# Two loads per head tied to a later store: the x1 loads of a hybrid decoder layer on one Trainium2 core

## The chip, the cores and the metric

The kernel runs on one core of one Trainium2 chip. The metric is device time in microseconds (us). Before the change it was timed three times: 1514.49, 1511.58 and 1510.92 us, median 1511.58 us. The profiled execution, a run of its own, took 1510.96 us.

## The reference

One decoder layer over 1024 tokens of 1024 features in float32. Two groups of heads, a chunked mLSTM and a forgetting attention, run on the same normalised input; their joined result goes through `w_out` and is added to x. Then comes a cross-attention into 256 memory tokens, and then a squared-ReLU MLP, each with its own pre-norm and residual:

```python
x = x + jnp.concatenate([ml_out, fx_out], axis=-1) @ w_out[l]
x = x + cross_attention(rmsnorm(x, ln_x[l]), rmsnorm(mem, ln_mem[l]), w_xq[l], w_xkv[l], w_xo[l])
u = jax.nn.relu(rmsnorm(x, ln2[l]) @ w_ff1[l])
x = x + (u * u) @ w_ff2[l]
return rmsnorm(x, ln_f)
```

In `cross_attention` the queries are `h @ w_q` for four heads of 256 features; keys and values come from the memory tokens; scores, softmax, weighted values and `w_xo` follow. The change touches how the sum of the first line ("x1" below, the first result) gets from DRAM to the place where the queries are made.

## The kernel before

**Layout.** Activations are stored feature-major: a tile is 128 features by 512 tokens. There are 8 feature tiles (KT) and two halves of 512 tokens (`hf` 0 and 1). A float32 product is made of three matmuls: every operand is cut into a high and a low part in the `fp32r` type (`split`, lines 131 to 138: ScalarE copies the high part, VectorE subtracts it to leave the low part), and `mm3` (lines 184 to 188) multiplies low by high, high by low and high by high into one PSUM bank.

**The end of the first result.** `w_out` is applied in two pieces. The first piece is added to x earlier and stored to the DRAM buffer `x1d`. The loop at lines 1139 to 1149 does the second: for `n0` in 0 and 4, for both halves, for four tiles `n`, nine matmuls make one tile in PSUM, and `full_sink` (line 1122) finishes it. It loads the partial sum from `x1d` into a buffer that comes in turn from `p`, `d`, `e` (line 1125), adds the PSUM bank (line 1126), and stores the sum back to the same place of `x1d` (line 1127). For the first half it also cuts the scaled sum into `h2`, which stays in SBUF. For the second half nothing stays in SBUF: the sum is only in `x1d`. `square_sum` adds the squares for the norm. So there are 16 stores; the last four are tiles 4, 5, 6 and 7 of the second half. `mix_done` holds the store of tile 5 (n == KT - 3) of the second half.

**The cross-attention's first half.** The loop at line 1451 runs over the four heads. For each head, `query_whole` multiplies two blocks of `w_xq` by `h2` (24 matmuls each, into the PSUM banks `mm` and `m2`, 512 tokens of the first half) and evicts them with a scaled split into the buffers `b`, `c` or `p`, `a`/`y` (line 1198). `right_side(hd)` prepares the second half, and `cross_head(hd, 0, ...)` does scores, softmax and values for the first half with the keys and values of its head, loaded at lines 1276 and 1277.

**The second half's query combinations.** The queries of the second half are made by a Strassen-like scheme with seven products per pair of blocks (`query_blocks`, line 1231), and these need seven right-hand sides: blocks 11, 21, 22 of the scaled x1 and the combinations t1, t2, t3, t4. `right_side(k)` (line 1168) makes the part of feature tiles k and 4 + k: it loads the two tiles `x` and `y` of x1 from `x1d` (line 1176) into the two buffers of the tag `f`, scales them by `ln_x` on ScalarE (line 1177), cuts three blocks, makes the differences on GpSimd (`sub`, line 1339) in place, and cuts those too; the last difference goes to the tile `fourth`. The four calls, one for each head, use the same two `f` buffers, so each call's loads wait until the one before is done with them. `query_blocks` starts after the loop over the heads and uses all of them.

**Queues and order.** All DMAs named here are issued by SyncE (SP), one after the other: a load whose condition isn't met keeps what stands behind it in SP's queue waiting. The conditions are semaphores put in where data or a buffer is shared; a load from `x1d` waits for the store to the same place to have landed. `tc.issue_after(ins)` is another thing: it waits for nothing by itself, and only says that what is issued in its block stands behind `ins` in the queue of the same engine. Here the order in which an engine gets its instructions is not written out by hand, unlike in the parts under `in_order`: the framework lays out the instructions of every engine when the program is built, with a timing model of its own (`schedule_with_timeline_sim=True`, line 1843). The weights come through the two buffers `wr` (line 174) and are cut into the three buffers each of `wh` and `wl`.

Of the kernel before, what the change touches and what calls it, by code (L numbers as in the profile page):

```python
# [21 lines left out]
KT = D // P  # L22
# [22 lines left out]
def hybrid_layer(ctx: ExitStack, tc: tile.TileContext, a: dict, out: bass.AP):  # L45
# [26 lines left out]
    def w4(shape=(P, 1024), dt=F32):  # L72
        t = sb("w4", [P, 1024], 5, dt)[: shape[0]]
        return t.rearrange("p (a b) -> p a b", b=shape[2]) if len(shape) == 3 else t
# [4 lines left out]
    def w2(tag, n=512, dt=F32, p=P):  # L79
        return sb("r_" + tag, [P, 512], BUFS[tag], dt)[:p, :n]  # L80
# [50 lines left out]
    def split(hi, lo, src, scale=None):  # L131

        if scale is None:
            s.activation(hi, src, AF.Copy)  # L134
            return v.tensor_tensor(out=lo, in0=src, in1=hi.bitcast(F32), op=ALU.subtract)  # L135
        else:
            s.activation(hi, src, AF.Copy, scale=scale)
            return v.scalar_tensor_tensor(out=lo, in0=src, scalar=scale, in1=hi.bitcast(F32), op0=ALU.mult, op1=ALU.subtract)  # L138
# [24 lines left out]
    def rotate(*tags):  # L163

        spare[tags] = spare.get(tags, -1) + 1
        return w2(tags[spare[tags] % len(tags)])
# [52 lines left out]
    def square_sum(acc, x, first, by=s, add=v):  # L219
        sq = acc if first else w2("c")[:, : x.shape[-1]]  # L220
        if by is s:
            s.activation(sq, x, AF.Square)
        else:
            by.tensor_tensor(out=sq, in0=x, in1=x, op=ALU.mult)
        if not first:
            add.tensor_tensor(out=acc, in0=sq, in1=acc, op=ALU.add)
# [872 lines left out]
    n = 0  # L1099
# [14 lines left out]
    banks[:] = ["mm", "tp", "m2", "tp"]  # L1114
    h2 = act(), act()
    x1_accs = [w2("b"), w2("b")]
    mix_done = []

    def ln_x(n):
        return vec[:, VEC["ln_x"] + n :][:, 0:1]  # L1120

    def full_sink(n, hf, ps):
        t = rotate("p", "d", "e")
        with tc.issue_after(last_raw[0].ins):
            load(t, x1d[hf, :, n])
        v.tensor_tensor(out=t, in0=ps, in1=t, op=ALU.add)
        done = load(x1d[hf, :, n], t)
        if hf == 0:
            split(h2[0][:, n], h2[1][:, n], t, ln_x(n))
        square_sum(x1_accs[hf], t, n == 0, add=g)  # L1130
        if hf == 1 and n == KT - 3:
            mix_done.append(done)

    def row_second(hf):
        rsqrt_sums(x1_accs[hf], rcol[:, 4 * hf : 4 * hf + 4], 4)
        if hf:
            to_row(row, rcol, 8, rowd[2:3])

    for n0 in (0, 4):
        ws = [weights(a["w_out_b"][n0 // 2 + i], 6 * P) for i in range(2)]  # L1140
        for hf in range(2):
            for n in range(n0, n0 + 4):
                w = both(ws[n // 2 % 2], lambda t: t.rearrange("p (k c) -> p k c", k=3)[:, :, n % 2 * P : n % 2 * P + P])
                ps = mm()
                for k in range(3):
                    mm3(ps, both(w, lambda t: t[:, k]), mix_fx[hf][k], k == 0, k == 2)
                full_sink(n, hf, ps)
                if hf and n == 6:
                    row_second(0)
# [7 lines left out]
    def right_room(*names):  # L1157
        t = act().rearrange("p a b -> p (a b)").rearrange("p (n q k c) -> p n q k c", n=2, q=2, k=4)
        for e, c in enumerate(names):
            R[c] = t[:, e, 0], t[:, e, 1]  # L1160
        return t[:, 1]

    def cut_right(c, k, x):
        split(R[c][0][:, k], R[c][1][:, k], x)
# [3 lines left out]
    def right_side(k):  # L1168
        if not fourth:
            for c in (("11", "21"), ("t1", "t2"), ("22", "t3")):  # L1170
                right_room(*c)
            fourth.append(w4((P, 4, 256)))
        x, y = w2("f"), w2("f")
        for t, n in ((x, k), (y, 4 + k)):
            with tc.issue_after(mix_done[0].ins):
                load(t, x1d[1, :, n])
            s.activation(t, t, AF.Copy, scale=ln_x(n))
        x1, x2, y1, y2 = (t[:, e * 256 : e * 256 + 256] for t in (x, y) for e in range(2))
        cut_right("11", k, x1)
        cut_right("21", k, y1)  # L1180
        cut_right("22", k, y2)
        sub(x1, x2, x1, g)
        cut_right("t1", k, x1)
        sub(x1, y2, x1, g)
        cut_right("t2", k, x1)
        sub(x2, y2, x2, g)
        cut_right("t3", k, x2)
        sub(fourth[0][:, k], y1, x1, g)
# [149 lines left out]
    def sub(out_, x, y, by=v):  # L1338
        by.tensor_tensor(out=out_, in0=x, in1=y, op=ALU.subtract)
# [111 lines left out]
    for hd in range(XH):  # L1451
        q = query_whole(hd)
        right_side(hd)
        if hd == XH - 1:
            last_room = right_room("t4")
            for k in range(4):
                cut_right("t4", k, fourth[0][:, k])
            for _ in range(2):
                left_query(*x_prep.pop(0))
        for _ in cross_head(hd, 0, q, *os_[0]):  # L1460
            pass
        if hd == 0:
            row_second(1)
# [384 lines left out]
```

## Time and profile before

| | us |
|---|---|
| median of three runs | 1511.58 |
| lowest, highest | 1510.92, 1514.49 |
| profiled execution, its own time | 1510.96 |
| span of the profiled execution | 1509.2 |
| busy in the span: DVE, ACT, POOL | 1122.7, 757.7, 528.7 |

The mean granted clock of TensorE in the profiled execution is 0.997 of full speed. The end of the first result's loop is at about 627 us of the span, the heads of the cross-attention's first half run from about 628 to 692 us, and the second half's queries begin behind that.

How to read the profile: PE is TensorE's matmul, PEld its weight load, DVE VectorE, ACT ScalarE, POOL GpSimd, SP SyncE with its DMA queue. Times in a timeline are microseconds from the start of the span; a row gives start, duration, engine, line of the kernel, operation, and "output<-inputs" by the names of the tiles (`act`: large activation tiles; `wr`, `wh`, `wl`: raw, high and low weights; `r_x`: the buffers of the tag x; `m`, `mm`, `tp`, `sc`, `ov`: PSUM banks, where `m` is the bank m2; `w`: the tiles of the tag w4). A number in square brackets is the idle time of the engine before the row and what ended it. A row of the waits reads: who waited for whom, microseconds in all, times, longest. A row of the chain of waits gives start, duration and what the time was spent in.

### The profile page before, as it was taken

The page shows a single profiled execution, that of the slowest core. Times are in us where ns is not written, and L with a number is a line of the kernel's source. Part 1 is how long each engine was busy: PE and PEld are TensorE (multiplying, and loading weights), DVE is VectorE, ACT ScalarE, POOL GpSimd, SP SyncE. Part 2 cuts the span into 40 slices and gives each one's busy share as a digit, 9 for nine tenths or more (in the row PEclk, how much of TensorE's full clock was granted, in tenths as well). Part 3 has the DMA queues.
Part 4 walks back from the last instruction along what each step waited for, and adds up shares of the span by engine and source line. Part 5 has one row for each costly group of instructions (what it writes and reads, how often), then busy time and mean ns, then how long its engine had stood idle before and what let it go on. Part 6 is the DMA issues. An engine that isn't in the chain of part 4 may idle for free.

```text
span 1509.2 us, 22358 instructions
## 1 busy us (share of the span) xinstructions
PE 1493.0 (99%) x7806; PEld 1263.7 (84%) x7806; DVE 1122.7 (74%) x1803; ACT 757.7 (50%) x1440; POOL 528.7 (35%) x545
## 2 busy tenths in 40 slices
PE   9999999999999999999999999999999999999997
PEld 9988888889899888788988878888888888888887
DVE  7766676664788875667767899989996678787765
ACT  7324343334688764566654467566664521122134
POOL 1003030414365441623300044454544365553312
PEclk9999999999999999999999999999999999999999
DMA  6322333435777877853354447676678677776623
GB/s 243 115 79 95 98 108 126 132 129 153 247 261 256 284 248 246 271 169 126 128 182 159 147 155 279 235 261 248 217 273 292 264 279 279 279 272 251 247 88 112
DMA packets 124276, 303.04 MB, mean 201 GB/s; under 512 B 13810, under 2 KB 28460, under 8 KB 117252
## 3 DMA queue, kind: packets, MB, share of 16 engines
q1 hardware_dynamic: 124164, 301.62, 57.3%
q8 instruction: 61, 1.00, 0.3%
q14 instruction: 51, 0.42, 0.1%
HBM read 202.75 MB, written 98.82 MB: 200 GB/s over the span
## 4 chain that ended last, share of the span: by engine, by line
PE 90%; DMA 4%; DVE 3%; ACT 1%; issue 1%; POOL 1%; POOLq 0%; DVEq 0%; SPq 0%; ACTq 0%
PE tp L186 8%; PE tp L187 8%; PE tp L188 8%; PE sc L186 6%; PE sc L188 6%; PE sc L187 6%; PE mm L186 5%; PE m L188 5%; PE m L186 5%; PE m L187 5%; PE mm L188 5%; PE mm L187 5%; PE ov L801 2%; PE ov L186 2%; PE ov L187 2%; PE ov L188 2%
## 5 line engine op out<-in xcount | busy, mean ns | idle before, releaser
L186 PE MATMUL tp<-act,wl 128*128 128x512 f32 (+1 forms) x440 | 172.6, 392 | 0.0
L187 PE MATMUL tp<-act,wh 128*128 128x512 f32 (+1 forms) x440 | 172.1, 391 | 0.0
L188 PE MATMUL tp<-act,wh 128*128 128x512 f32 (+1 forms) x440 | 171.8, 392 | 0.0
L135 DVE TENSOR_TENSOR wl<-wr,wh 128x1024 fp32r<-128x1024 f32 (+2 forms) x99 | 131.4, 1327 | 27.0 <-ACT wh L134 26.7
L134 ACT ACTIVATE wh<-wr 128x1024 fp32r<-128x1024 f32 (+2 forms) x99 | 99.8, 1008 | 85.7 <-PE tp L188 32.7
L186 PE MATMUL mm<-act,wl 128*128 128x512 f32 (+1 forms) x332 | 124.8, 376 | 2.6 <-DVE r_c L138 2.1
L188 PE MATMUL mm<-act,wh 128*128 128x512 f32 (+1 forms) x332 | 124.1, 374 | 0.0
L187 PE MATMUL mm<-act,wh 128*128 128x512 f32 (+1 forms) x332 | 123.8, 373 | 0.0
L186 PE MATMUL m<-act,wl 128*128 128x512 f32 (+1 forms) x308 | 113.8, 369 | 0.6 <-DVE wl L135 0.6
L188 PE MATMUL m<-act,wh 128*128 128x512 f32 (+1 forms) x308 | 113.8, 369 | 0.0
L187 PE MATMUL m<-act,wh 128*128 128x512 f32 (+1 forms) x308 | 113.7, 369 | 0.0
L188 PE MATMUL sc<-act,wh 128*128 128x512 f32 (+1 forms) x280 | 105.6, 377 | 0.0
L187 PE MATMUL sc<-act,wh 128*128 128x512 f32 (+1 forms) x280 | 105.6, 377 | 0.0
L186 PE MATMUL sc<-act,wl 128*128 128x512 f32 (+1 forms) x280 | 105.6, 377 | 0.0
L1612 POOL TENSOR_TENSOR z<-wr 128x256 f32<-128x256 f32 x56 | 52.9, 966 | 131.8 <-DMA wr<-w_ff2q 126.7
L188 PEld LDWEIGHTS tp<-act,wh 128*128 128x128 f32 x440 | 82.7, 188 | 19.0
L186 PEld LDWEIGHTS tp<-act,wl 128*128 128x128 f32 x440 | 82.7, 188 | 18.5
L187 PEld LDWEIGHTS tp<-act,wh 128*128 128x128 f32 x440 | 82.7, 188 | 18.2
L134 ACT ACTIVATE wh<-z 128x1024 fp32r<-128x1024 f32 (+1 forms) x54 | 55.5, 1027 | 81.8 <-POOL z L1612 62.3
L135 DVE TENSOR_TENSOR wl<-z,wh 128x1024 fp32r<-128x1024 f32 (+1 forms) x54 | 77.7, 1439 | 11.4 <-ACT wh L134 11.4
L134 ACT ACTIVATE w<-wr 128x768 fp32r<-128x768 f32 (+3 forms) x35 | 28.0, 801 | 107.4 <-PE tp L186 33.0
L186 PEld LDWEIGHTS mm<-act,wl 128*128 128x128 f32 x332 | 62.7, 189 | 14.2 <-DVE r_c L138 2.6
(734 smaller groups left out, 4387.2 us busy)
## 6 DMA issues: line engine op xcount, KB each, us to landing
act<-right SPq DMA_DIRECT2D x49, 1024.0 KB
right<-w SPq DMA_DIRECT2D x56, 256.0 KB
wr<-w_ff2q SPq DMA_DIRECT2D x28, 512.0 KB
right<-r_d SPq DMA_DIRECT2D x49, 256.0 KB
right<-r_e SPq DMA_DIRECT2D x49, 256.0 KB
act<-fqk SPq DMA_DIRECT2D x48, 256.0 KB
wr<-w_in SPq DMA_DIRECT2D x20, 512.0 KB
wr<-w_ff SPq DMA_DIRECT2D x20, 512.0 KB
```

What stands on the lines that cost most here:

```text
L134: s.activation(hi, src, AF.Copy)
L135: return v.tensor_tensor(out=lo, in0=src, in1=hi.bitcast(F32), op=ALU.subtract)
L186: nc.tensor.matmul(ps, w[1], x[0], start=first, stop=False, skip_group_check=more)
L187: nc.tensor.matmul(ps, w[0], x[1], start=False, stop=False, skip_group_check=more)
L188: nc.tensor.matmul(ps, w[0], x[0], start=False, stop=last, skip_group_check=more)
L801: nc.tensor.matmul(self.ov[:, c0:], self.fv[:, self.j], t[:, c0:], start=self.j == 0 and t is self.p[1], stop=self.last and t is self.p[0])
L1612: g.tensor_tensor(out=o, in0=x, in1=y, op=op)
```

## The change

A second list, `x1_done`, holds the store of tile 7 of the second half, the last of the 16 stores. The loads of x and y in `right_side` are tied to that store in place of the store of tile 5 (`mix_done`). The loads of keys and values in `cross_head` stay tied to `mix_done`.

```diff
-    mix_done = []
+    mix_done, x1_done = [], []
...
         if hf == 1 and n == KT - 3:
             mix_done.append(done)
+        if hf == 1 and n == KT - 1:
+            x1_done.append(done)
...
         for t, n in ((x, k), (y, 4 + k)):
-            with tc.issue_after(mix_done[0].ins):
+            with tc.issue_after(x1_done[0].ins):
                 load(t, x1d[1, :, n])
             s.activation(t, t, AF.Copy, scale=ln_x(n))
```

## The prediction

> **What bounds the kernel now.** I read the page's head first, for the span and the share of each engine.
>
> ```profile
> span 1509.2 us, 22358 instructions
> PE 1493.0 (99%) x7806; PEld 1263.7 (84%) x7806; DVE 1122.7 (74%) x1803; ACT 757.7 (50%) x1440; POOL 528.7 (35%) x545
> ```
>
> TensorE (PE) is busy for 1493.0 of 1509.2 us, so the whole span holds 16.2 us of PE idle time. A gain can only come out of that idle time and out of stretches with a lowered clock. Next I read the busy time by stage around the moved loads (span of the stage; then PE, PEld, DVE, ACT, POOL busy; then granted clock, DMA share, GB/s), and who made PE wait from 560 to 900 us.
>
> ```profile
> 640.00:645.00 5.00, 3.26 (x9) 2.59 (x10) 4.73 (x6) 3.69 (x7) 1.52 (x2) 0.75 0.66 235
> 645.00:650.00 5.00, 5.00 (x29) 4.35 (x29) 0.90 (x3) 1.30 (x3) 0.73 (x1) 0.91 1.00 378
> ```
>
> ```profile
> PE mm L186 <- DVE r_c L138: 2.1, 1, 2.1
> PE m L186 <- DVE wl L135: 0.6, 1, 0.6
> PE mm L186 <- DVE wl L135: 0.4, 1, 0.4
> ```
>
> The longest of these waits, 2.1 us, falls in the first of the two stages, and the clock is lowered behind it: 5 x (1 - 0.75) + 5 x (1 - 0.91) = 1.25 + 0.45 = 1.7 us of work lost. So this spot costs 2.1 + 1.7 = 3.8 us. Beside it PE waits there only 0.4 and 0.6 us. The two chains that lead into the 2.1 us come from SP's queue in order of time, and from the chain of waits.
>
> ```profile
> 626.28 0.37 SPq L1127 DMA_DIRECT2D x1d<-r_p  x1
> 626.87 0.32 SPq L1127 DMA_DIRECT2D x1d<-r_d  x1
> 627.24 4.13 SPq L1176 DMA_DIRECT2D r_f<-x1d  x2
> 631.47 0.38 SPq L174 DMA_DIRECT2D wr<-w_xq  x1
> 631.96 0.36 SPq L1127 DMA_DIRECT2D x1d<-r_e  x1
> 632.41 0.38 SPq L1127 DMA_DIRECT2D x1d<-r_p  x1
> 635.25 0.33 SPq L174 DMA_DIRECT2D wr<-w_xq  x1
> 635.68 0.38 SPq L1276 DMA_DIRECT2D w<-kxd  x1
> 636.12 0.42 SPq L1277 DMA_DIRECT2D w<-vxd  x1
> 641.70 0.32 SPq L1176 DMA_DIRECT2D r_f<-x1d  x1
> ```
>
> ```profile
> 626.28 4.76 DMA x1d<-r_p
> 631.05 3.82 DMA r_f<-x1d
> ```
>
> The 16 results of full_sink go through the buffers p, d, e in turn. Counted back from the last store (r_p, 632.41: tile 7 of the second half), 631.96 is tile 6, 626.87 is tile 5 (the one in mix_done), and 626.28 is tile 4. The two L1176 loads at 627.24 are x (tile 0) and y (tile 4). x issues at once; y must wait until the store of tile 4 has landed, 4.76 us after its issue, and so stands at the head of SP's queue until 631.05. Behind it stand a weight load and the last two stores. y lands 3.82 us later. From there the work goes through ACT and DVE:
>
> ```profile
> 634.90 0.73 ACT L1177 ACTIVATE r_f<-r_f,vec 128x512 f32<-128x512 f32 x1 [0.93 <-DMA r_f<-x1d]
> ...
> 639.74 0.42 ACT L134 ACTIVATE act<-r_f 128x256 fp32r<-128x256 f32 x1 [0.53 <-POOL r_f L1339]
> 640.18 0.60 ACT L137 ACTIVATE r_b<-mm 128x512 fp32r<-128x512 f32 x1
> ```
>
> ```profile
> 639.20 0.39 PE L188 MATMUL m<-act,wh 128*128 128x512 f32 x1
> 641.74 0.50 PE L186 MATMUL mm<-act,wl 128*128 128x512 f32 x1 [2.14 <-DVE r_c L138]
> ```
>
> ACT does its list in order. The eviction of the first query projection (L137, r_b<-mm) stands behind four cuts of right_side(0) and the GpSimd (POOL) subtractions between them, so PE gets the bank mm back late. This is the 2.14 us.
>
> **The change, part by part.** It adds no instruction and takes none away: eight L1176 loads now have to stand behind the store of tile 7 in SP's queue. The last six stand behind it already (641.70 and later), so only x and y of right_side(0) move.
>
> What goes away: y's wait at the head of the queue (631.05 - 627.24 - 0.32 = 3.5 us). By the time tile 7 is stored, tile 4 has long landed. The weight load of 631.47 could issue about 3.4 us earlier and the two stores some 0.6 us earlier. I cost that at nothing gained: the cut of that weight is put behind r_b<-mm on ACT in any case, and the stores themselves are bound by their own additions:
>
> ```profile
> 631.07 0.68 DVE L1126 TENSOR_TENSOR r_p<-tp,r_p 128x512 f32<-128x512 f32 x1
> ```
>
> What is added: the last store can't issue before 631.07 + 0.68 = 631.75. With 0.38 for it and 0.4 for x ahead, y issues at about 632.55 in place of 631.05, 1.5 us late, and x at 632.15 in place of 627.24. With the same 3.82 us to land, ACT's L1177 for y moves from 634.90 to 636.4. That is the price I take: +1.5 us on the chain of the right sides. Bounds: where y lands as quickly as the load of 666.4 further down (its ACT user starts at 669.83, 3.4 us after its buffer came free), +1.1; nothing can make it a gain, since the last store's own addition ends behind 631.05. Where the weight load of 635.25 and the two loads of 635.68 and 636.12 (512 KB each) are put ahead of x and y, their 1.5 MB at the 350 GB/s of a full DMA stage is 4.3 us more: +5.8.
>
> ```profile
> 635.00:640.00 5.00, 4.59 (x20) 3.38 (x18) 3.96 (x8) 2.74 (x7) 3.04 (x3) 1.00 1.01 350
> ```
>
> The order of the compute engines here isn't written out by hand; it is laid down when the program is built, by a timing model (line 1843). With x and y later, the eviction r_b<-mm can come ahead of some or all of the cuts in ACT's list. At the end of m (639.20 + 0.39) PE then finds the bank free and the 2.1 + 1.7 us vanish at this place. The question is what is late next. I followed what is behind it in the timelines of ACT and POOL and in the chain of waits:
>
> ```profile
> 650.64 0.72 ACT L1177 ACTIVATE r_f<-r_f,vec 128x512 f32<-128x512 f32 x1 [2.94 <-DMA r_f<-x1d]
> ...
> 653.01 0.99 POOL L1339 TENSOR_TENSOR w<-r_f,r_f 128x256 f32<-128x256 f32 x1
> ...
> 665.64 0.74 POOL L1339 TENSOR_TENSOR w<-r_f,r_f 128x256 f32<-128x256 f32 x1
> ...
> 669.83 0.73 ACT L1177 ACTIVATE r_f<-r_f,vec 128x512 f32<-128x512 f32 x1 [3.81 <-DMA r_f<-x1d]
> ```
>
> ```profile
> 698.13 4.61 DMA wr<-w_xq
> 702.77 1.07 ACT wh L134
> 703.86 1.44 DVE wl L135
> 705.34 0.38 PE mm L186
> ```
>
> The two r_f buffers come free with the last subtraction of each right side, and the next pair of loads waits for it (653.01 + 0.99 = 654.0 and 665.64 + 0.74 = 666.4). So right_side(0) sets right_side(1), and so on to right_side(3). ACT waits 2.94 and 3.81 us for those loads, its weight cuts stand behind them, the cuts free the weight buffers, and at 705.34 PE waits 0.4 us for the last of these. This chain is made of loads, cuts and subtractions; PE's own pace enters little. If PE comes to it 3.8 us early it waits there instead, and if the chain is 1.5 us late, PE is late by that as well.
>
> The sum, either way: PE's start at 705.34 moves by the chain's +1.5. If the stall stays at 641.74 and grows, that is all: +1.5. If it moves to 705, the idle time there is 0.4 + 3.8 + 1.5 = 5.7 us, and the clock falls behind it as it did behind the 2.1 us. That loss of 1.7 us comes after the point that the chain sets, and so it is added: +3.2. I take the second, since x lands so much later that I expect the order on ACT to change. From there to 900 PE has only the 0.6 us of wait to absorb it, so the shift reaches the end: 1510.96 (the profiled execution: its span of 1509.2 and 1.8 around it) + 3.2 = 1514.2. The median of the runs, 1511.58, is 0.6 above that execution; I leave this to the range.
>
> The clock row stands against a rule of the Trainium skill, page "TensorE: Matmul & The Clock Gate", part on the HAM clock gate: the clock is halved after about an idle window of 3.4 us. Here 2.14 us was enough, so the measurement decides; by the rule a stall kept under 3.4 us would lose no clock, and its removal would be worth 2.1 us in place of 3.8, while the 5.7 us at 705 would lose it under both.
>
> **The rivals.** (1) The stall goes and doesn't come back: the eviction gets ahead of the cuts and the chain to 705 has room that I don't see, 3.8 us or more. For it: the chain of waits goes through PE's own work from 641.74 to the start of this row, so some of it may follow PE's pace.
>
> ```profile
> 641.74 0.50 PE mm L186
> 662.49 0.68 DVE r_y L138
> ```
>
>  Against: ACT's waits of 2.94 and 3.81 us for the r_f loads. Time: 1510.96 - 3.8 = 1507.2; with the 0.4 and 0.6 us too, 1506.2. It decides if PE arrives at its first block of the second head's queries before 702. (2) The key and value loads get ahead of x and y: +5.8, or +7.5 with the clock loss: 1516.8 to 1518.5. For it: they are tied to tile 5 still, as x and y no longer are. Against: before, the program put them behind the last store. (3) Nothing to see: the compute order stays and y lands as fast as the bound of +1.1, or the chain has just that room: 1511 to 1512.1. The rule "behind tile 7" is an order in one queue, and y moves little.
>
> **How the numbers follow.** Forecast (+1.5 to +3.2) 0.38, rival 1 0.20, rival 2 0.32, rival 3 0.10. The bound of 0.3% is 4.5 us, about what a measurement of this kernel can tell from no change: 1507.0 to 1516.1. Faster by more: rival 1 where it takes one of the small waits along, 0.13. Slower by more: rival 2 whole, and 0.13 of the forecast for a further wait that the new order brings: 0.45. Within: 0.42. The forecast's own range is 1512.0 to 1516.0; with most of rival 1 and of rival 2 the range is 1507.2 to 1519.5, which leaves some 0.1 below and 0.1 above.
>
> **What would show it.** In SP's queue the weight load of 631.47 near 628 and no wait in front of L1176, x and y just behind the last store near 632 to 633: the change does what it says. ACT's L1177 for y at 636 to 637: the 1.5 us. r_b<-mm ahead of cuts, no PE wait near 640 and one of 4 to 6 us with a lowered clock near 700: the stall has moved. No wait in either place: rival 1, and I am wrong about the chain. Key and value loads ahead of x in SP's queue: rival 2. A wait of PE at a place that these rows don't name would show that the new order, and not the loads, decides.

## The result and the profile after

| | before | after |
|---|---|---|
| median of 22 runs, us | 1511.78 | 1513.95 |
| lowest, highest | 1509.40, 1515.04 | 1511.40, 1516.09 |
| profiled execution, its span | 1510.96, 1509.2 | 1514.38, 1512.6 |

The ratio after to before is 1.0012 (95% interval 1.0007 to 1.0018): 1.1 to 2.7 us slower. It is a small loss, inside the prediction's bound of 0.3%.

The head of the page after, then who made PE wait from 600 to 900 us (who waited for whom, us in all, times, longest):

```profile
span 1512.6 us, 22358 instructions
PE 1493.2 (99%) x7806; PEld 1264.1 (84%) x7806; DVE 1121.6 (74%) x1803; ACT 758.6 (50%) x1440; POOL 530.4 (35%) x545
```

```profile
PE sc L186 <- DVE r_c L138: 3.8, 1, 3.8
PE m L186 <- DVE wl L135: 0.7, 1, 0.7
PE mm L186 <- DVE r_c L138: 0.6, 1, 0.6
```

The wait of 2.1 us is down to 0.6, and a new one of 3.8 us has come, at another instruction. The timeline of PE gives both places, and the windows (span; PE, PEld, DVE, ACT, POOL busy; clock, DMA share, GB/s) give the clock:

```profile
641.80 0.50 PE L186 MATMUL mm<-act,wl 128*128 128x512 f32 x1 [0.60 <-DVE r_c L138]
659.87 0.58 PE L186 MATMUL sc<-w,r_c 128*128 128x256 f32 x1 [3.76 <-DVE r_c L138]
```

```profile
640.00:645.00 5.00, 4.40 (x20) 3.25 (x19) 3.92 (x7) 3.03 (x7) 3.24 (x4) 1.00 0.20 47
...
655.00:660.00 5.00, 1.24 (x6) 0.69 (x4) 5.00 (x10) 1.92 (x5) 3.21 (x4) 0.98 0.59 208
660.00:665.00 5.00, 5.00 (x18) 4.11 (x19) 1.38 (x6) 4.59 (x12) 0.01 (x1) 0.68 0.36 117
...
690.00:710.00 20.00, 20.00 (x145) 18.63 (x144) 15.71 (x30) 14.89 (x37) 9.30 (x8) 1.00 0.45 151
```

From 640 to 645 the clock is whole now; from 655 to 665 it is lowered, and 5 x 0.02 + 5 x 0.32 = 1.7 us of work are lost. From 690 to 710, where the prediction looked for the stall, PE is busy all the time. Waits and clock together, before: 2.1 + 0.6 + 0.4 + 1.7 = 4.8 us. After: 3.8 + 0.7 + 0.6 + 1.7 = 6.8. That is +2.0, about what the medians differ by (2.2). The two profiled spans differ by 3.4; 1.6 of that is there when PE comes to the first wait (641.80 - 0.60 = 641.20 against 641.74 - 2.14 = 639.60). Up to 626 us all engines, and up to 644 us PE, have their instructions in the same order in both kernels, so I don't count it to the change. (Over all eleven kernels below, with the same order up to there, the profiled executions come to this place from 0.3 us sooner to 3.1 us later than the one before.)

Where the new wait comes from is read backwards. First SP's queue after:

```profile
633.73 0.32 SPq L1127 DMA_DIRECT2D x1d<-r_p  x1
634.10 1.07 SPq L1178 DMA_DIRECT2D r_f<-x1d  x2
636.38 6.90 SPq L174 DMA_DIRECT2D wr<-w_xq  x2
643.38 0.37 SPq L1278 DMA_DIRECT2D w<-kxd  x1
643.80 0.42 SPq L1279 DMA_DIRECT2D w<-vxd  x1
645.02 0.80 SPq L1178 DMA_DIRECT2D r_f<-x1d  x2
```

x and y of right_side(0) stand behind the last store, as the change asks. But another thing has moved too. In the kernel before, one weight load (635.25) stood ahead of head 0's key and value loads (635.68, 636.12). Now there are two in a row. The second has to wait for a raw weight buffer, so the queue stands still for 6.90 us. The key and value loads, 1 MB, go out at 643.4 to 643.8, straight ahead of x and y of right_side(1). The consequence on ACT and DVE, and one row of the chain of waits:

```profile
640.11 0.60 ACT L137 ACTIVATE r_b<-mm 128x512 fp32r<-128x512 f32 x1
...
650.30 0.73 ACT L1179 ACTIVATE r_f<-r_f,vec 128x512 f32<-128x512 f32 x1 [4.23 <-DMA r_f<-x1d]
652.70 0.73 ACT L1179 ACTIVATE r_f<-r_f,vec 128x512 f32<-128x512 f32 x1 [1.67 <-DMA r_f<-x1d]
...
656.77 0.42 ACT L134 ACTIVATE act<-r_f 128x256 fp32r<-128x256 f32 x1 [1.16 <-POOL r_f L1341]
657.09 0.58 ACT L137 ACTIVATE r_b<-mm 128x512 fp32r<-128x512 f32 x1
```

```profile
659.14 0.68 DVE L138 SCALAR_TENSOR_TENSOR r_c<-mm,r_b 128x512 fp32r<-128x512 f32 x1
```

```profile
645.44 7.18 DMA r_f<-x1d
```

The last of the two loads needs 7.18 us to land. For y of right_side(1) that is not new: in the kernel before it was issued behind 1 MB of keys and values of head 1 and a weight load, and was scaled 7.1 us later (at 650.64, a row that the prediction shows).

```profile
643.53 0.38 SPq L1176 DMA_DIRECT2D r_f<-x1d  x1
```

After the change ACT waits 4.23 and 1.67 us for the two loads, and behind their cuts and a subtraction of POOL stands the eviction of head 1's first query block (657.09). PE is through with head 1's second query block at 656.1 (659.87 - 3.76), and its next work, the scores of head 1, needs r_c (659.14), which DVE makes behind that eviction. It is the same pattern as before, an eviction on ACT behind the cuts of a right side; one head later, and longer.

How much of the 3.76 us is PE coming early, and how much is r_c coming late? Two rows of the kernel before allow an estimate:

```profile
655.19 0.69 DVE L138 SCALAR_TENSOR_TENSOR r_c<-mm,r_b 128x512 fp32r<-128x512 f32 x1
657.42 0.28 PE L186 MATMUL sc<-w,r_c 128*128 128x256 f32 x1
```

I count from where PE runs into its first wait (639.60 before, 641.20 after), which leaves the 1.6 us out. Before, r_c was ready 16.3 us on (655.88) and PE came for it 17.8 us on: 1.5 us of room. After, PE is through 14.9 us on, 2.9 us sooner, and r_c is ready 18.6 us on (659.82), 2.3 us later. So 2.9 - 1.5 = 1.4 us of the wait would have come with r_c as it was before: this part is the stall of 641 coming back. The other 2.3 us are the new order's: y of right_side(1) is scaled 0.5 us later, the eviction is 0.9 us later (it started at 654.57 before), and DVE, which made r_c right after the eviction before, now has cuts and a maximum in between, 1.4 us more.

### The profile page after: what moved, and what is told of

Read it like the earlier page. It is cut to its first block, busy times and chain, and to the rows that moved or that the text cites. A ratio compares the mean times of both kernels' runs of the same rounds, so it can differ in the third digit from the quotient of the medians.

```text
span 1512.6 us, 22358 instructions
## 1 busy us (share of the span) xinstructions
PE 1493.2 (99%) x7806; PEld 1264.1 (84%) x7806; DVE 1121.6 (74%) x1803; ACT 758.6 (50%) x1440; POOL 530.4 (35%) x545
## 4 chain that ended last, share of the span: by engine, by line
PE 92%; DMA 3%; DVE 2%; ACT 1%; issue 1%; SPq 0%; POOL 0%; POOLq 0%; DVEq 0%; ACTq 0%
PE tp L186 8%; PE tp L187 8%; PE tp L188 8%; PE sc L186 7%; PE sc L188 7%; PE sc L187 7%; PE m L186 6%; PE m L188 6%; PE m L187 6%; PE mm L186 5%; PE mm L188 5%; PE mm L187 5%; PE ov L801 2%; PE ov L186 2%; PE ov L187 2%; PE ov L188 2%
```

## The experiments

Two theories were set against each other. The prediction's: loads, cuts and subtractions of the right sides bound PE near 700, so what is gained at 641 is paid back there. The other, formed from the trace after: the time is set by the order that is laid out when the kernel is built, above all by what stands ahead of a right side's loads in SP's queue, and by what stands ahead of a query block's eviction on ACT. Times are medians in us; the ratio compares each kernel with runs of before that were made beside it, and the last two columns are of the one profiled execution.

| kernel | time | ratio to before (95%) | PE's waits 600 to 900 us | work lost to a lowered clock, us |
|---|---|---|---|---|
| before | 1511.78 | | 3.1 | 1.7 |
| after | 1513.95 | 1.0012 (1.0007 to 1.0018) | 5.1 | 1.7 |
| e1 | 1513.29 | 1.0010 (1.0001 to 1.0018) | 4.6 | 0 |
| e2 | 1512.65 | 1.0004 (0.9995 to 1.0014) | 6.3 | 0 |
| e3 | 1507.36 | 0.9967 (0.9954 to 0.9979) | 0.9 | 0 |
| e4 | 1510.35 | 0.9990 (0.9982 to 0.9999) | 2.3 | 0 |
| e5 | 1508.62 | 0.9979 (0.9969 to 0.9989) | 1.9 | 0 |
| e6 | 1512.25 | 1.0003 (0.9994 to 1.0013) | 3.9 | 0 |
| e7 | 1513.57 | 1.0010 (1.0002 to 1.0019) | 3.8 | 0 |
| e8 | 1513.34 | 1.0007 (0.9999 to 1.0016) | 6.3 | 0 |
| e9 | 1511.05 | 0.9998 (0.9989 to 1.0007) | 2.7 | 0 |

The time less waits and clock is 1506.4 to 1509.8 in all eleven. That is a spread of 3.4 us: the two columns account for e3 and e5 against the changed kernel, but not for differences of 1 to 2 us among the others.

Tying only the loads of right_side(0) to the last store, or tying the key and value loads to it as well, gives the same program as the change, so there is no run of these.

### e1: only y tied to the last store

```diff
-            with tc.issue_after(x1_done[0].ins):
+            with tc.issue_after((x1_done if n > 3 else mix_done)[0].ins):
```

> Only y (tiles 4 to 7) stands behind the last store, x (tiles 0 to 3) stays behind tile 5. The weight load and the two stores are then free of y's wait as in the changed kernel, but the queue behind them keeps the order of before: key and value loads ahead of the next but one weight load. Theory A (the moved wait near 656 us comes from SP's queue: the key and value loads of head 0 stand behind a weight load that waits 6.9 us for its buffer, and push the loads of right_side(1)): no PE wait of over 1.5 us near 656; y is still some 1.5 to 3 us late, ACT still has the eviction behind all cuts, so the wait near 641 grows from 2.1 to 3.6 to 5 us with the lowered clock behind it: 1513 to 1515 us. Theory B (the lateness of y alone sets the loss, whatever the queue): the same 1513 to 1515 us, but with a wait near 656 too. Theory C (the new order of the compute engines makes the loss): the order is that of before, so 1511.5 us.

y is scaled at 636.44, 1.5 us later than before, but the key and value loads stay early (636.34, 636.77) and there is no stall near 656. The wait at 641 is 0.9 us, and the clock stays whole. Theory A had that wait grow to 3.6 to 5 us with the later y; it fell. The chain of waits of before shows why y alone doesn't set it: between y's scaling and the first subtraction stand a square on ACT (635.84) and its sum on POOL (636.60, 1.29 us), which the prediction's reading left out. In e1 the square stands ahead of y's scaling (634.84). Still the time is 1.5 us above before (0.2 to 2.7 by the interval). Part of what was gained at 641 is lost further down: PE waits 1.4, 1.2 and 0.9 us, the first of these at 697:

```profile
697.37 0.38 PE L186 MATMUL sc<-w,r_y 128*128 128x256 f32 x1 [1.42 <-DVE r_y L138]
```

But waits and clock together are 4.6 us against 4.8 before, so they don't account for the loss of 1.5 us, and the rest isn't located. The wait at 697 looks like the prediction's payment near 700. e9 asks whether the right sides make it.

### e9: e1, with one scaling behind an eviction on ACT

```diff
             scaled = s.activation(pr[:, i], pr[:, i], AF.Copy, scale=rden[:, i : i + 1])
+            if (hd, hf) == (2, 0):
+                scalings.append(scaled)
...
                 split(*t, ps, 1.0 / 16.0)
+                if (hd, kk) == (3, 0):
+                    for scaled in scalings:
+                        tc.add_manual_dep(scaled.ins, evicted.name, ...)
```

> The kernel of e1 with one more order on ACT: the scaling of head 2's softmax (z<-z,c_rden, 687.40 in e1) stands behind the eviction of head 3's first query block (r_b<-mm, 689.01 in e1), as it does in the kernel before and in e3. The compute and the right sides are the same up to there. Theory that the chain to 690 to 710 goes through PE's scores, the softmax and this eviction: r_b<-mm comes 1.7 us sooner, the weight load behind it too (near 690.2 in place of 691.87), r_y comes near 695, PE's wait of 1.42 us at 697.37 falls under 0.4, and the time to 1510.5 to 1512.2 in place of 1513.3. Rival (the prediction's: loads, cuts and subtractions of the right sides set this stretch): they are as in e1, so PE waits there as long, 1512.7 to 1514.

ACT in e1, then in e9, and the windows from 690 to 710 of e1 and of e9:

```profile
687.40 1.71 ACT L1298 ACTIVATE z<-z,c_rden 128x256 f32<-128x256 f32 x4 [1.28 <-DVE c_rden L1296]
689.01 0.58 ACT L137 ACTIVATE r_b<-mm 128x512 fp32r<-128x512 f32 x1
```

```profile
687.29 0.60 ACT L137 ACTIVATE r_b<-mm 128x512 fp32r<-128x512 f32 x1
688.68 1.71 ACT L1309 ACTIVATE z<-z,c_rden 128x256 f32<-128x256 f32 x4 [0.79 <-DVE c_rden L1307]
```

```profile
690.00:710.00 20.00, 18.58 (x139) 17.38 (x138) 15.33 (x28) 13.76 (x32) 4.30 (x3) 1.00 0.42 133
```

```profile
690.00:710.00 20.00, 20.00 (x152) 18.82 (x150) 15.64 (x28) 14.49 (x33) 5.36 (x4) 1.00 0.44 133
```

One edge on ACT, and the 1.42 us of idle PE are gone. Up to 687 us the compute engines have the same order in e1 and e9; behind it more has moved, and a wait of 1.22 us at 723 is gone too, while the one at 641 is 0.7 us longer. The medians differ by 2.2 us, the ratios by 1.8, and the two intervals overlap. The right sides are no earlier: their last subtraction starts at 677.46 in e9 and at 676.13 in e1. So they don't make this wait; the place of the eviction on ACT does. One detail came out otherwise than expected: the weight load was no sooner (692.67 against 691.87), since the cut that frees its buffer now stands behind the scaling. It was r_y, at 693.86 in place of 696.63, that came sooner.

### e3: the changed kernel, with the second weight load put back behind the key and value loads

```diff
+    def query_weights(hd, kk):
+        if (hd, kk) != (2, 1):
+            return weights(a["w_xq"][2 * hd + kk])
+        with tc.issue_after(kv_loads[0].ins):
+            raw = weight_load(a["w_xq"][2 * hd + kk])
+        return weight_parts(raw)
```

(`kv_loads` holds head 0's value load.)

> The changed kernel, and the second weight load of head 2 put behind the value load of head 0 in SP's queue, so the key and value loads of head 0 don't stand behind its wait. Theory A: those loads issue near 636 to 638 in place of 643.4, the loads of right_side(1) land 1.5 to 2.5 us earlier than at 650.2 and 652.6, the PE wait of 3.8 us near 656 falls under 2 us, and the time is 1509.5 to 1512 us. Theory B: y of right_side(0) is as late as before, the wait stays near 3 us, 1513 to 1514.5 us. Theory C: the eviction now stands one cut further ahead on ACT, which takes 0.4 us off the wait: 1513 to 1514 us.

SP's queue in e3, then ACT:

```profile
635.51 0.33 SPq L174 DMA_DIRECT2D wr<-w_xq  x1
635.94 0.38 SPq L1291 DMA_DIRECT2D w<-kxd  x1
636.37 0.42 SPq L1292 DMA_DIRECT2D w<-vxd  x1
643.75 0.80 SPq L1178 DMA_DIRECT2D r_f<-x1d  x2
```

```profile
647.58 1.53 ACT L1179 ACTIVATE r_f<-r_f,vec 128x512 f32<-128x512 f32 x2 [2.78 <-DMA r_f<-x1d]
...
651.16 0.58 ACT L137 ACTIVATE r_b<-mm 128x512 fp32r<-128x512 f32 x1
```

The key and value loads are out 7.4 us sooner, right_side(1)'s loads are scaled at 647.58 in place of 650.30 and 652.70, and head 1's eviction comes at 651.16 in place of 657.09. PE has waits of 0.7 and 0.2 us left, and the longest pieces of its chain of waits from 640.5 to 712 are all PE's own. One edge in SP's queue, with the new order of PE, ACT and DVE behind it that comes along, is worth 6.6 us against the changed kernel, and this version is 0.33% faster than before. That is more than theory A had forecast (1509.5 to 1512).

### e4: the changed kernel, with right_side(1)'s scaling behind head 1's eviction on ACT

```diff
-            s.activation(t, t, AF.Copy, scale=ln_x(n))
+            scaled = s.activation(t, t, AF.Copy, scale=ln_x(n))
+            if k in (1,):
+                tc.add_manual_dep(scaled.ins, evicted[0].name, ...)
```

> The changed kernel, and on ACT the eviction of head 1's first query block put ahead of right_side(1)'s scaling and cuts; SP's queue is as in the changed kernel, so the loads stay late. If the chain of loads, cuts and subtractions bounds PE further down (as the prediction had it for 705 us), the wait near 656 goes and one of 2 to 5 us comes at 680 to 706, 1512 to 1515 us. If only the place of the eviction on ACT made the wait, it goes and nothing comes back: 1508 to 1510 us.

The loads stay late (keys and values at 642.22, x and y scaled at 650.24 and 652.00), but the eviction is at 649.75, ahead of them, and the wait near 656 is gone with its clock: 1510.35, 3.6 us under the changed kernel and just above the 1508 to 1510 of the second theory. So the new stall needs both, loads that land late and an eviction queued behind them. A wait of 1.0 us has come at 681, less than the 2 to 5 us that the first theory asked for.

### e5, e6, e7: the kernel before, with its own stall taken away

e5 is the kernel before with the same edge for head 0 (`if k in (0,)`): right_side(0)'s scaling stands behind the eviction that PE waited 2.14 us for.

> The kernel before (x and y behind tile 5), and on ACT the eviction of head 0's first query block put ahead of right_side(0)'s scaling and cuts: the wait near 641 is taken away without moving x and y to the last store. The program's order then puts the second weight load of head 2 ahead of the key and value loads of head 0 in SP's queue, as in the changed kernel. Theory A (that order sets the wait near 656): no wait near 641, key and value loads issue after 641, a PE wait of 2.5 to 5 us near 656 with a lowered clock, 1511 to 1515 us. Theory D (tying x and y to the last store is itself what makes right_side(1) late, and with x and y early it is on time): no wait near 656, 1507 to 1509 us.

1508.62, 3.0 us under the runs of before beside it (1511.65). The stall at 641 is gone, and nothing came back near 700. But PE waits 1.07 us at 655.43, for r_c at the scores of head 1, where the changed kernel has its 3.76. SP's queue and ACT in e5:

```profile
635.36 4.63 SPq L174 DMA_DIRECT2D wr<-w_xq  x2
640.09 0.37 SPq L1287 DMA_DIRECT2D w<-kxd  x1
...
644.63 0.94 SPq L1176 DMA_DIRECT2D r_f<-x1d  x2
```

```profile
647.74 0.72 ACT L1177 ACTIVATE r_f<-r_f,vec 128x512 f32<-128x512 f32 x1 [0.73 <-DMA r_f<-x1d]
```

The two weight loads stand ahead of the key and value loads here too, so that order alone doesn't make a stall of 3.8 us. But the buffer came free after 4.63 us, the key and value loads had 4.5 us of lead on right_side(1)'s in place of 1.6, and x was scaled at 647.74. So the order by itself doesn't say how late a load lands; when the queue gets to it has to be read as well.

e6 is e5 with e3's edge as well.

> As the run with the eviction of head 0 ahead, and that second weight load of head 2 put behind the value load of head 0. Theory A: key and value loads issue near 636, no PE wait over 1 us near 641 or 656, 1506.5 to 1509 us, so the changed edge for x and y isn't needed for the gain. Theory D: the same 1507 to 1509 us as without this edit. If the gain of the run with the key and value loads first needs x and y behind the last store, a wait of 2 us or more stays and the time is 1510 us or more.

1512.25, above what theories A and D forecast. The key and value loads do go early (636.81), but the rest was laid out anew, with waits of 1.8 us of m for its weights, 1.4 and 0.7. In its queue y of right_side(2) stands behind a weight load (658.89), and I put the loss down to that. e7 is e6 with that weight load behind y.

> The kernel of e6 with one more order in SP's queue: the weight load that stood between x and y of right_side(2) (658.47 there, y at 658.89) now stands behind y; the compute is the same. Landing theory (what a right side's loads find ahead of them in SP's queue decides, through ACT's cuts, when PE gets its next buffers): y issues together with x near 656, up to 3 us sooner, the last subtraction of right_side(2) ends near 667 in place of 668.91, the waits of m for wl fall from 1.8 to under 0.8 us, and the time comes back by 1.5 to 3.5 us: 1508.5 to 1510.8. Rival (e6 is slow for the new order of the compute engines as a whole): 1511.5 to 1513.5, with the waits in other places.

1513.57, above the range of either theory: PE, ACT, DVE and POOL have e6's order throughout, x and y now go one behind the other, but y waits for its own buffer (2.86 us for the two) and gets out no sooner, and the waits of m for its weights are 2.2 us. So this run doesn't test whether e6 loses by y's place in the queue. Why the layouts of e6 and e7 lose what e5 gained stays open; e7's time less its waits, 1509.8, is the highest of all, so part of its loss shows in no wait of its profiled execution.

### e2 and e8: tied to the store of tile 6

```diff
-        if hf == 1 and n == KT - 1:
+        if hf == 1 and n == KT - 2:
```

e2 is the changed kernel with this, e8 is e3 with it.

> x and y stand behind the store of tile 6, and ahead of the store of tile 7. Theory A: the key and value loads are ahead of the blocked weight load, so no wait over 1.5 us near 656; the eviction stands behind four cuts in place of three, so about 1 us of wait near 641, and the time is 1510 to 1512 us. Theory B: y late by about 1 us less than in the changed kernel, a wait of 2 to 3 us near 656, 1512 to 1513 us. Theory C: the order of ACT differs from both; it says only that the time is not that of either.

> The kernel of e3 with the loads tied to the store of tile 6 in place of tile 7. SP's queue then has x and y of right_side(0) one store sooner, but y of right_side(1) behind the key and value loads of head 1 (1 MB more ahead of it); the compute is the same. Landing theory: y of right_side(1) reaches ACT some 3 us later than in e3, the last subtraction of right_side(1) ends near 656 in place of 652.91, and PE waits for it by 710: 1509 to 1511.5. Rival 1 (the order of the weight load against head 0's key and value loads is all that matters): as e3, 1506.5 to 1508.3. Rival 2 (the prediction's +1.5 us of a later y still counts, so an earlier store saves it): 1505.5 to 1506.5.

e2 (1512.65) has no large stall but five waits of 0.9 to 1.5 us: theory A's wait at 641 is there (1.06 us), one of 1.28 at 656 too, and the time is above its range. In e8 y of right_side(1) stands behind head 1's keys and values:

```profile
644.63 0.32 SPq L1178 DMA_DIRECT2D r_f<-x1d  x1
645.04 0.38 SPq L1291 DMA_DIRECT2D w<-kxd  x1
645.52 0.38 SPq L1292 DMA_DIRECT2D w<-vxd  x1
645.99 0.38 SPq L1178 DMA_DIRECT2D r_f<-x1d  x1
```

```profile
652.24 0.72 ACT L1179 ACTIVATE r_f<-r_f,vec 128x512 f32<-128x512 f32 x1 [1.41 <-DMA r_f<-x1d]
```

y is scaled at 652.24, where e3 had both done by 649.1. The place and the lateness are as expected; the price, 6 us above e3, is more than the 1.5 to 4 I had given it, because waits of 1.7 us at 642, 1.6 at 700 and 1.1 at 725 came along with the new layout: the compute is not in e3's order, as I had expected it to be. An earlier store saved nothing.

## Why the prediction came out as it did

The time (1514.2 against 1513.95) and the sign hold. The way there holds in part, and the closeness of the number is luck.

- **What it removes and adds.** Held: y's wait at the head of SP's queue is gone; the last store, x and y follow one another. e1 shows y alone late: 636.44 against 634.90, 1.5 us, of which 0.4 are there when PE runs into its first wait. In the changed kernel y is scaled at 638.44, 3.5 us later, of which 1.6 are there at that place.
- **The stall at 641 goes, with its clock.** Held: 2.1 to 0.6 us, granted clock 0.75 to 1.00 from 640 to 645. The eviction stands behind three cuts now; it was five before (635.53 to 639.74), not the four that the prediction counts.
- **It comes back at 705, because the right sides bound PE there.** This is the step that failed ("This chain is made of loads, cuts and subtractions; PE's own pace enters little. If PE comes to it 3.8 us early it waits there instead"). In e3 PE comes to 640 without a stall, the last subtraction of right_side(3) starts at 678.99, no earlier than before (678.50), and PE still gets through 690 to 710 without a wait. What failed is that the prediction let the order change at 641 and kept the old one for what comes behind. Before, the weight cut on ACT did stand behind the scaling of right_side(3), which waited 3.81 us for its load (669.83). In e3, and in every other kernel here, it stands ahead of it. Before, then e3:

```profile
672.93 1.06 ACT L134 ACTIVATE wh<-wr 128x1024 fp32r<-128x1024 f32 x1
```

```profile
669.37 1.06 ACT L134 ACTIVATE wh<-wr 128x1024 fp32r<-128x1024 f32 x1
...
670.79 1.34 ACT L1179 ACTIVATE r_f<-r_f,vec 128x512 f32<-128x512 f32 x2
```

The rest of the chain to 705 moves with PE. The softmax of head 2 reads scores (sc) that PE made; before, then e3:

```profile
685.81 0.56 ACT L1293 ACTIVATE z<-sc,c_mx,rcol 128x256 f32<-128x256 f32 x1 [3.32 <-DVE c_var L198]
```

```profile
682.90 0.57 ACT L1308 ACTIVATE z<-sc,c_mx,rcol 128x256 f32<-128x256 f32 x1 [3.54 <-DVE c_var L198]
```

PE's scores came 2.4 us sooner in e3 and the softmax 2.9, and with it the eviction and the weight cut behind it. The prediction drew on ACT's waits for the r_f loads alone; this wait of 3.32 us, ended by DVE and not by a load, was in the trace of before. The chain of waits of before takes another branch here: POOL's subtractions of weights (683.06), c_y (686.92) and DVE's r_c (689.56). All three come 2.9 to 3.0 us sooner in e3 as well, and there the first of them follows right behind right_side(3)'s last subtraction, so 3 us is about the room that the right sides left. That the chain would have had it with the order of before is not shown: no other run keeps that order.
- **In its place:** a stall of 3.8 + 1.7 us at the scores of head 1. By the estimate above 1.4 us of the wait are the prediction's own mechanism, PE coming early to a right side's eviction, but at right_side(1) and not at 705; 2.3 us are r_c's being later in the new order. e3 (loads earlier) and e4 (eviction ahead of them) each take the whole stall away, and e2, e5, e6, e7 and e8 have a wait of 0.7 to 1.4 us at the same instruction. The prediction's last sentence on what would show it wrong named this case: a wait at a place that the rows don't name, so that the new order decides. Its sum was 5.7 + 1.7 at 705, less the 0.4 there and the 3.8 at 641 before: +3.2. Measured were 3.8 + 1.7 at 656 and 0.6 left at 641, 0.1 more at 870, less the same 4.2: +2.0. That the sums lie close is chance: e1, e2 and e8, with the same loads moved, have other stalls in other places.
- **Rival 1** (the stall goes and doesn't return, 1507.2) was wrong for this kernel, but e3 (1507.36) and, but for 1.1 us at 655, e5 (1508.62) are that case in other orders. **Rival 2** had the right actors and the wrong order: the key and value loads didn't get ahead of right_side(0)'s loads, they fell back onto right_side(1)'s. **Rival 3** didn't occur: the compute order did change.
- **The clock.** Windows laid on it show one stretch of 3.4 us at half the clock in each of the two profiled executions, 1.7 us of work. (The clock falls once more at the end of the program, in all eleven.) Before, then after:

```profile
642.46:645.88 3.42, 3.42 (x11) 2.65 (x10) 2.59 (x4) 2.10 (x4) 0.00 (x0) 0.50 0.87 287
```

```profile
659.80:663.22 3.42, 3.35 (x9) 2.79 (x10) 1.15 (x6) 2.81 (x10) 0.20 (x1) 0.50 0.59 199
```

2.14 us of idle PE stand ahead of it before, 3.76 us after. Behind the 1.71 us of e8 the clock is whole:

```profile
642.59 0.50 PE L186 MATMUL mm<-act,wl 128*128 128x512 f32 x1 [1.71 <-DVE r_c L138]
```

```profile
640.00:645.00 5.00, 3.29 (x14) 2.37 (x13) 4.55 (x7) 4.00 (x7) 4.09 (x4) 1.00 0.45 180
```

No threshold follows from these single executions. One such stretch takes 1.7 of some 1512 us, 0.0011 of the mean granted clock, and over the runs of before that mean goes from 0.995 to 0.998. The nine kernels whose profiled execution has no such stretch have 0.997 or 0.998 there. But in e7, one of these, four of twelve runs have 0.996; they took 1515.2 us on average, the other eight 1512.5. So the same program seems to pay such stretches in some executions and not in others, and the column of the table holds for one execution. The Trainium skill ("TensorE: Matmul & The Clock Gate", part on the HAM clock gate) has the clock halved after an idle window of about 3.4 us: the 3.76 us after agree with that, the 2.14 us before were enough without it.

What stays open: which rule of the layout put the second weight load ahead, why e6 and e7 lose, where e1 loses what its waits don't hold, and what decides whether a stall lowers the clock. A third raw weight buffer, which might take the wait of 6.90 us away altogether, wasn't tried.

## What to carry to other kernels

Where the order of all engines is laid out by a model at build time, an edge that moves two loads can move any other instruction: look in the new program's queues for what has changed places before pricing the edge, and pin the order that matters (here one edge in SP's queue, 6.6 us; the same edge on another order, e6 against e5, cost 3.6) rather than hope for it. A load that waits for its buffer holds up everything behind it in its queue (6.90 us here). Before saying that a chain has no room, ask of each wait on it what ended it: one that another engine's data ended can move with that engine. And where the change may move instructions, a chain read in the old order is no bound for the new one.

## What was not expected of the hardware

That 2.14 us of idle PE were enough for 3.4 us at half the clock, and that runs of one program seem to differ in it. And the landing time of a 256 KB load behind others: 3.82 us for y of right_side(0) in the kernel before, about 7.1 us for y of right_side(1) behind 1 MB of keys and values and a weight load (643.53 to 650.64), and 7.18 us after the change, issued 1.6 us behind 1 MB of keys and values (645.44 against 643.80).
